# A streaming encoder layer on one Trainium2 core: a reordered LoRA, stores and loads on other queues, two-input work moved between engines, and a new step table

## The chip, the core and the metric

One core of one Trainium2 chip. The core has a matrix engine (TensorE, "PE" in the profile; its weight loads are "PEld"), a vector engine (VectorE, "DVE"), an activation engine (ScalarE, "ACT"), a general engine (GpSimd, "POOL") and a queue engine for transfers (SyncE, "SP"). ACT and POOL can issue transfers too; an engine takes its instructions in order, issues of transfers included, and "ACTq", "POOL ... DMA" or "SPq" in a row is such an issue. The metric is the device time of one execution in microseconds (us), lower is better.

## The reference, cut to what matters

One layer works on 1056 token rows (1024 of a prompt, 32 of running streams). One input projection feeds three mixers, whose outputs are concatenated, projected, normalised, and followed by an MLP.

```python
proj = x @ prm['w_in']
q_lat, kv_lat, k_rope_raw, u, p_rwkv = jnp.split(proj, IN_SPLITS, axis=-1)
mla_out, ckv, krope = mla_mixer(q_lat, kv_lat, k_rope_raw, pos, ckv_past, krope_past, prm)   # 6 heads
s5_out, s5_state = s5_mixer(u, s5_x0, s5_block_len, prm)
rwkv_out, rwkv_state, shift = rwkv_mixer(p_rwkv, shift0, rwkv_s0, prm)                       # 6 heads x 64
merged = jnp.concatenate([mla_out, s5_out, rwkv_out], -1)                                    # 384 | 256 | 384
x = layer_norm(ALPHA * x + merged @ prm['w_out'], ...)
x = layer_norm(ALPHA * x + jnp.square(jax.nn.relu(x @ prm['w_up'])) @ prm['w_down'], ...)

# in rwkv_mixer: a LoRA of three parts (32, 32 and 64 inner columns)
w_log = -jax.nn.softplus(-(prm['w0'] + jnp.tanh(wd) @ prm['w_w2'])) - 0.5
a = jax.nn.sigmoid(prm['a0'] + ad @ prm['w_a2'])
g = jax.nn.sigmoid(gd) @ prm['w_g2']
...
bonus = jnp.sum(r * k * prm['r_k'], -1, keepdims=True) * v
y = (y + bonus.reshape(b, t, RWKV_W)) * g
# in s5_mixer
z = jax.nn.gelu(y);  out = z * jax.nn.sigmoid(z @ prm['w_glu'] + prm['b_glu'])
# in mla_mixer: q = rms_norm(q_lat) @ w_qb; 64 plain ("nope") and 32 rotated ("rope") columns a head
```

## The kernel before

**Numbers.** Most products are made in three passes over a value split in a high and a low part: `split3` (L45 to L50) copies the high part on ScalarE (L49) and subtracts it on VectorE, or on an engine given as `lo_eng` (L50); `mm3` (L59 to L67) multiplies hi by hi (L63), lo by hi (L65) and hi by lo (L67).

**Input stage (0 to some 270 us).** Tiles of 128 columns of the input projection (`in_proj`, results "acc") run in turn, each over three blocks of 384, 384 and 288 tokens. `stage_lora` computes, for each of three pairs of RWKV heads and each of three blocks (384, 384, 290 columns), a gate (64 rows of weights, bank "pti") and the two 32-row products `w` and `a` (banks "fs" or "pt"), each in three passes (L308). A chain of `issue_after` fixes the order gate, w, a in every pass. ScalarE empties the banks with sigmoids (L310 to L313). After the last sigmoid ScalarE changes its function table (L76), and `front_k` (L351 to L403, VectorE and ScalarE) and the triangular inverse (`rwkv_inv`, L770 to L826) follow. `stage_kv_in`, `stage_kr`, `stage_q_in`, `stage_u` and `stage_q` finish the projections. `stage_q` (L1169) makes the queries and stores them in DRAM as `q_d`, per head 64 nope rows (`nope(p)` for heads 2p and 2p+1, L1182, from ScalarE) and 32 rope rows (L1196 and L1204, from POOL). After it the "shift" output (`sho`) is transposed and stored (L2263 to L2266).

**The middle (some 270 to 690 us).** Four generators are interleaved: F (`attn_front`: keys, query loads, score maxima), O (`attn_back`: values, scores, softmax times values), S (the inverse's end, then the RWKV scan in nine tiles of 128 tokens) and X (`stage_s5`). The string `PLAN` gives the order: each letter lets one generator run to its next `yield`. The function `middle` ties the TensorE instructions of a step behind those of the step before (`mark`), so TensorE's order is the table's; the other engines' orders come from the compiler's own schedule, made with estimated times. What the prediction touches here: `attn_setup` clears and copies key tiles on POOL (L1111 to L1118) and zeroes 32 rows of the two query pairs `q2` on ScalarE (L1120); `attn_keys` (L1128) makes the keys of two heads from one bank at a time; `attn_q` (L1212) loads a head's query from `q_d` and splits it; `attn_max` takes the maxima of the scores (L1235, L1236); in `attn_out`, `ptk` clears on POOL (L1292) precede the `av` products (L1265), and L1270 to L1278 finish a block. In the scan, `rwkv_pairs` (L863, L864) and `rwkv_norm` (L1003, L1004) have two POOL instructions each. In `stage_s5`, the results are written to `z_d` (L673), read back in another layout by sixteen loads on SP (L688), and passed through the GELU on ScalarE (L693).

**Output projection (some 640 to 790 us).** `out_early` loads and splits three token tiles (384 columns) of the merged results `mg_d` with POOL while attention runs out. The last attention store is put in `g.late` (L814) and issued after it (L2288). Then come six more tiles: `out_load` (L1452) loads `mraw` and splits it with POOL, `out_mm` multiplies, `out_ln` and `out_turn` normalise and transpose. The MLP fills the rest of the time; nothing of it is changed.

Of the kernel before, what the change touches and what calls it, by code (L numbers as in the profile page):

```python
# [277 lines left out]
def stage_lora(g):  # L278
# [15 lines left out]
    for p in PAIRS:  # L294
        cs = slice(p * P, p * P + P)
        nc.gpsimd.memset(g.cs65[:, p, 0:1040].rearrange("p (c x) -> p c x", x=65)[:, :, 0:1], 0.0)
        nc.gpsimd.memset(g.cs65[:, p, 1040:1041], 0.0)
        nc.gpsimd.memset(g.at[:, p, 1024:1026], 0.0)
        gt = g.lq.tile([P, WSH], F32, tag="o", name="gt", bufs=2)
        for i, (s, n) in enumerate(HB):  # L300
            pool, tag = ((g.pfs, "fs"), (g.pt, "pt"))[(p + i) % 2]
            w, a = (pool.tile([P, 512], F32, tag=tag, name=tag)[:, :n] for _ in range(2))
            gate = g.pti.tile([P, 512], F32, tag="pti", name="pti")[:, :n]
            mm = None
            for j, (l, r) in enumerate(((wh_, ah), (wh_, al), (wl_, ah))):
                for z, rows in ((gate, slice(64, 128)), (w, slice(0, 32)), (a, slice(32, 64))):
                    with g.tc.issue_after(mm.ins) if mm is not None else nullcontext():
                        mm = nc.tensor.matmul(out=z, lhsT=l[rows, cs], rhs=r[rows, s:s + n], start=j == 0, stop=j == 2)  # L308
# [304 lines left out]
def stage_s5(g):  # L613
# [72 lines left out]
    for h in range(2):  # L686
        for i in range(8):
            nc.sync.dma_start(out=zv[16 * i:16 * i + 16, h], in_=g.z_d[8 * h + i].rearrange("(t c) k -> c t k", c=16))  # L688
# [297 lines left out]
def rwkv_norm(g, t):  # L986
# [16 lines left out]
    nc.gpsimd.tensor_tensor(out=yc, in0=yc, in1=g.bn.pop(t), op=ALU.add)  # L1003
    nc.gpsimd.tensor_tensor(out=yc, in0=yc, in1=gate, op=ALU.mult)  # L1004
# [148 lines left out]
def stage_q(g):  # L1153
# [24 lines left out]
    def nope(p):
        q = f("qnope")
        product(q, wa[:, :, 2 * p:2 * p + 2].rearrange("p k h c -> p k (h c)"))  # L1180
        for h in range(2):
            nc.scalar.dma_start(out=g.q_d[2 * p + h, 0:64], in_=q[hsl(h)])  # L1182
# [12 lines left out]
    for h in range(4):  # L1195
        nc.gpsimd.dma_start(out=g.q_d[h, 64:96], in_=qa[32 * h:32 * h + 32])  # L1196
# [135 lines left out]
def middle(g, scan):  # L1332
# [39 lines left out]
    "FFFFFFFFFFFSFFFFFFSFFSFFFFFFFFFSFFFFSOOSOFSOOOSFOOSOOSOOSFSOSFOFOOOOOSSXOOOFSFOOSXOOOOFOOOSFFSSSOSSO"  # L1372
    "OXFFXFOSFOFOSOSXFFFOOFSOSSOSXOOSFSFSOOFSXOOSOFOFOSXSOOSFOOFXOXOSFOFSOOOOSFOFOSXOSSOOOFSOOXFSFOOSFFFS"
    "FXSFFFFSFFXSOOSFOSOOFOOOOSXFSSSOOXFOSOOSOOFXOOSOOFOOSXSSOFOOFOSOXOSSOOOOFOSXOFFSOXSFFSSFFFSFFSOOXSOS"
    "FFXSSFOOSOOOXOSOOOFSOOOOOSFOOSOFSXOOOFSSOXSOFFOOSFOOSXOOFSOSFXOOOOSSFOFSXFFFSFFFSFFFXSFFSFFSOOXOOSOS"
    "OOFSOXOSFFOSOSOXOFSOOFSOXOOSSXOSFOFOOOOOOOSFSSSOXSFOOOOSFOXFOXOSOSFOFOSSSFFSFFFFOOOOSOOOSOOOSOOOSOSS"
    "OOSSOOSOSFOSOOOOOOOOOOOOOOO"
# [806 lines left out]
def tile_trunk(ctx, tc, a, o):  # L2184
# [31 lines left out]
    with ExitStack() as s1:  # L2216
# [49 lines left out]
        nc.scalar.dma_start(out=g.o["sh_s"], in_=sho[10:20])  # L2266
# [146 lines left out]
```

## Time and profile before

| | us |
|---|---|
| median of 3 runs (lowest, highest) | 1465.21 (1462.29, 1467.37) |
| the profiled execution | 1463.32 |
| its span, first to last instruction | 1461.2 |
| busy: TensorE | 1381.3 (95%) |
| busy: VectorE | 970.7 (66%) |
| busy: ScalarE | 656.0 (45%) |
| busy: GpSimd | 161.9 (11%) |
| mean granted TensorE clock | 0.978 |

The page of the profile gives busy shares and the chain of work that ended last. The other views are of the same execution: stretches of the span with every engine's busy time, the timeline of one engine (start, length, engine, line, operation, written tile, read tiles, shapes, count; in brackets the idle time before and what ended it), and the list of waits (who waited for whom: total, times, longest). TensorE's matmuls are pipelined: its pace is read from starts, not lengths.

### The profile page before, as it was taken

What the parts mean: (1) busy time and instruction counts of PE and PEld (TensorE: products, weight loads), DVE (VectorE), ACT (ScalarE), POOL (GpSimd) and SP (SyncE); (2) the same over time, 40 slices, a digit from 0 to 9 for tenths busy, and PEclk for the clock granted to TensorE, in tenths of its full rate; (3) what the DMA queues carried; (4) which work ended last, traced back from release to release, by engine and by line L of the source; (5) the groups of instructions that cost most, each with busy time, mean ns of one, the idle gap of its engine ahead of it and who ended that gap; (6) DMA issues with size and microseconds to landing.
All of it is one profiled execution on the core that took longest, in us unless ns stands there. A gap on an engine that the chain in (4) does not pass through costs nothing.

```text
span 1461.2 us, 28203 instructions
## 1 busy us (share of the span) xinstructions
PE 1381.3 (95%) x11532; PEld 1236.2 (85%) x11532; DVE 970.7 (66%) x1735; ACT 656.0 (45%) x1143; POOL 161.9 (11%) x278
## 2 busy tenths in 40 slices
PE   9999999799989979889899899999999999999996
PEld 9978888476776757666589899999999999999996
DVE  7675979655664745652858976666656786665477
ACT  6546544335553645542326444344444344434432
POOL 1211110401111111210530000000000000000022
PEclk9999999899998999989999999999999999999998
DMA  5433563671343321131633344444429785354232
GB/s 202 146 123 135 168 172 87 168 138 50 92 107 87 82 60 35 64 108 44 214 119 131 136 181 139 162 142 147 137 87 385 256 306 187 90 172 131 70 101 76
DMA packets 150325, 198.58 MB, mean 136 GB/s; under 512 B 53392, under 2 KB 98116, under 8 KB 149688
## 3 DMA queue, kind: packets, MB, share of 16 engines
q1 hardware_dynamic: 129396, 175.91, 37.7%
q10 hardware_dynamic: 20448, 19.88, 4.5%
q8 instruction: 90, 1.47, 0.4%
q0 software_dynamic: 352, 1.01, 0.3%
q14 instruction: 39, 0.32, 0.1%
HBM read 129.42 MB, written 67.28 MB: 135 GB/s over the span
## 4 chain that ended last, share of the span: by engine, by line
PE 75%; DVE 9%; DMA 6%; ACT 4%; issue 2%; SPq 2%; ACTq 1%; POOL 1%; DVEq 0%; POOLq 0%
PE acc L63 19%; PE acc L67 19%; PE acc L65 19%; PE av L1265 3%; PE sc L63 1%; DMA mraw<-mg_d 1%; DVE mx L1236 1%; PE st L63 1%; DMA wo<-in_w_out 1%; PE st L65 1%; PE st L67 1%; PE scv L1147 1%; PE scq L1169 1%; PE pti L308 1%; PE sc L67 1%
## 5 line engine op out<-in xcount | busy, mean ns | idle before, releaser
L63 PE MATMUL acc<-xo,wo 128*128 128x272 f32 (+1 forms) x896 | 254.0, 284 | 2.8 <-ACT wo L49 2.8
L67 PE MATMUL acc<-xo,wo 128*128 128x256 f32 (+1 forms) x896 | 253.2, 284 | 1.6 <-DVE wo L50 1.6
L65 PE MATMUL acc<-xo,wo 128*128 128x272 f32 (+1 forms) x896 | 253.0, 283 | 0.0
L67 PE MATMUL acc<-hop,wo 128*128 128x272 f32 (+1 forms) x896 | 194.4, 284 | 0.0
L63 PEld LDWEIGHTS acc<-xo,wo 128*128 128x128 f32 x896 | 168.1, 188 | 3.0 <-ACT wo L49 3.0
L67 PEld LDWEIGHTS acc<-xo,wo 128*128 128x128 f32 x896 | 167.9, 188 | 2.0 <-DVE wo L50 2.0
L65 PEld LDWEIGHTS acc<-xo,wo 128*128 128x128 f32 x896 | 168.5, 188 | 0.0
L63 PE MATMUL acc<-hop,wo 128*128 128x256 f32 (+1 forms) x768 | 159.1, 285 | 0.0
L65 PE MATMUL acc<-hop,wo 128*128 128x272 f32 (+1 forms) x768 | 158.3, 283 | 0.0
L67 PEld LDWEIGHTS acc<-hop,wo 128*128 128x128 f32 x896 | 142.4, 188 | 0.0
L65 PE MATMUL acc<-xl,wmhi 128*128 128x384 f32 (+3 forms) x384 | 126.8, 330 | 0.7 <-DVE xl L50 0.7
L67 PE MATMUL acc<-xh,wmlo 128*128 128x384 f32 (+3 forms) x384 | 126.1, 329 | 0.0
L63 PE MATMUL acc<-xh,wmhi 128*128 128x384 f32 (+3 forms) x384 | 125.8, 328 | 0.3 <-ACT xh L49 0.3
L65 PEld LDWEIGHTS acc<-hop,wo 128*128 128x128 f32 x768 | 119.6, 189 | 0.0
L63 PEld LDWEIGHTS acc<-hop,wo 128*128 128x128 f32 x768 | 118.7, 188 | 0.0
L49 ACT ACTIVATE wo<-wr 128x512 fp32r<-128x512 f32 (+1 forms) x64 | 46.9, 738 | 117.6 <-PE acc L67 70.2
L2150 POOL TENSOR_TENSOR wr<-wr,gb 128x512 f32<-128x512 f32 (+1 forms) x12 | 17.2, 1453 | 667.7 <-ACT wr L2148 667.7
L1265 PE MATMUL av<-ptk,vo 128*128 128x512 f32 (+5 forms) x204 | 75.1, 452 | 11.7 <-ACT po L1270 8.1
L50 DVE TENSOR_TENSOR hop<-hraw,hop 128x1056 fp32r<-128x1056 f32 (+3 forms) x58 | 70.4, 1213 | 14.4 <-ACT hop L49 14.3
L50 DVE TENSOR_TENSOR wo<-wr,wo 128x512 fp32r<-128x512 f32 (+1 forms) x64 | 52.3, 821 | 40.7 <-ACT wo L49 40.6
L49 ACT ACTIVATE hop<-hraw 128x1056 fp32r<-128x1056 f32 (+3 forms) x58 | 60.6, 1045 | 30.2 <-PE acc L67 28.9
L65 PEld LDWEIGHTS acc<-xl,wmhi 128*128 128x128 f32 (+1 forms) x384 | 70.8, 184 | 3.9 <-DVE xl L50 1.3
(552 smaller groups left out, 3071.6 us busy)
## 6 DMA issues: line engine op xcount, KB each, us to landing
hraw<-h_d SPq DMA_DIRECT2D x48, 528.0 KB
wr<-in_w_up SPq DMA_DIRECT2D x35, 512.0 KB
h_d<-hx SPq DMA_DIRECT2D x16, 792.0 KB
h_d<-ht SPq DMA_DIRECT2D x16, 792.0 KB
wd<-in_w_dn SPq DMA_DIRECT2D x16, 512.0 KB
wr<-in_w_dn SPq DMA_DIRECT2D x16, 512.0 KB
ld<-rw SPq DMA_DIRECT2D x24, 320.0 KB
wmraw<-in_w_m SPq DMA_DIRECT2D x12, 512.0 KB
```

The source lines that it names most:

```text
L49: nc.scalar.activation(out=hi, in_=ps, func=AF.Copy)
L50: (lo_eng or nc.vector).tensor_tensor(out=lo, in0=ps, in1=hi.bitcast(F32), op=ALU.subtract)
L63: nc.tensor.matmul(out=outs[i], lhsT=lh, rhs=rhs[i][0], start=start, stop=False, **kw)
L65: nc.tensor.matmul(out=outs[i], lhsT=lh, rhs=rhs[i][1], start=False, stop=False, **kw)
L67: nc.tensor.matmul(out=outs[i], lhsT=ll, rhs=rhs[i][0], start=False, stop=stop, **kw)
L308: mm = nc.tensor.matmul(out=z, lhsT=l[rows, cs], rhs=r[rows, s:s + n], start=j == 0, stop=j == 2)
L1147: nc.tensor.matmul(out=ps[:n, j], lhsT=c, rhs=g.wkv[:, 1, p * P:p * P + P], start=True, stop=True)
L1169: nc.tensor.matmul(out=ps, lhsT=w[:, k], rhs=g.qn[:, k, s:s + n], start=k == 0, stop=k == 1)
L1236: nc.vector.tensor_reduce(out=mx[:n, t, b // 512:b // 512 + 1], in_=ps[:n, :w], axis=AX.X, op=ALU.max)
L1265: nc.tensor.matmul(out=po[:, c:n], lhsT=vo[:w, kt].rearrange("p a x -> p (a x)")[:, 64 * i:64 * i + P], rhs=pt[:w, c:n], start=kt == tiles ...
L2150: nc.gpsimd.tensor_tensor(out=o[:n, c], in0=o[:n, c], in1=g.gb2[:n, 0, c], op=ALU.mult)
```

## The change

- LoRA: in each of the nine groups the three passes of `w` and `a` are issued first, then the three of the gate, tied behind them.
- S5: the second eight of the sixteen loads of `z_d` are issued by POOL, and two more `yield`s stand before the GELU.
- The four POOL instructions of the scan, the low parts of `out_load`, and four clears in `attn_setup` go to VectorE.
- Only the first query pair is zeroed in `attn_setup`; the second is zeroed when head 1 loads its query.
- `attn_first_keys` replaces `attn_keys` for heads 0 and 1: four products into four banks, then the splits of head 0, then head 0's query, then the splits of head 1.
- Query stores: nope rows of heads 0 and 1 on SP, of heads 2 to 5 on POOL; rope rows of heads 0 to 3 on SP. The nope tiles lie in the memory of the input's low part.
- The last attention store is issued by ScalarE. The shift output is made ahead of `stage_u` and stored from SP.
- A new `PLAN` (526 letters for 527: three F steps fewer, two X steps more).

```diff
-            mm = None
-            for j, (l, r) in enumerate(((wh_, ah), (wh_, al), (wl_, ah))):
-                for z, rows in ((gate, slice(64, 128)), (w, slice(0, 32)), (a, slice(32, 64))):
-                    with g.tc.issue_after(mm.ins) if mm is not None else nullcontext():
-                        mm = nc.tensor.matmul(out=z, lhsT=l[rows, cs], rhs=r[rows, s:s + n], start=j == 0, stop=j == 2)
+            low = ((wh_, ah), (wh_, al), (wl_, ah))
+            for j, (l, r) in enumerate(low):
+                for z, rows in ((w, slice(0, 32)), (a, slice(32, 64))):
+                    mm = nc.tensor.matmul(out=z, lhsT=l[rows, cs], rhs=r[rows, s:s + n], start=j == 0, stop=j == 2)
+            for j, (l, r) in enumerate(low):
+                with g.tc.issue_after(mm.ins):
+                    mm = nc.tensor.matmul(out=gate, lhsT=l[64:128, cs], rhs=r[64:128, s:s + n], start=j == 0, stop=j == 2)
...
-            nc.sync.dma_start(out=zv[16 * i:16 * i + 16, h], in_=g.z_d[8 * h + i].rearrange("(t c) k -> c t k", c=16))
+            (nc.sync, nc.gpsimd)[h].dma_start(out=zv[16 * i:16 * i + 16, h], in_=g.z_d[8 * h + i].rearrange("(t c) k -> c t k", c=16))
...
+    yield
+    yield
     yield
     yield
     log_exp_table(g, [nc.scalar.activation(out=zt, in_=zt, func=AF.Gelu_apprx_tanh)], False)
...
-    nc.gpsimd.tensor_tensor(out=x, in0=ld[:, :, 2, :w], in1=ld[:, :, 4, :w], op=ALU.mult)
+    nc.vector.tensor_tensor(out=x, in0=ld[:, :, 2, :w], in1=ld[:, :, 4, :w], op=ALU.mult)
...
-    nc.gpsimd.tensor_tensor(out=yc, in0=yc, in1=g.bn.pop(t), op=ALU.add)
+    nc.vector.tensor_tensor(out=yc, in0=yc, in1=g.bn.pop(t), op=ALU.add)
...
-        for x in g.q2[i] if i < 2 else ():
+        for x in g.q2[i] if i < 1 else ():
...
+def attn_first_keys(g):
+    nc = g.nc
+    parts = []
+    for j, (src, o, n) in enumerate(((g.ckv[:, 0:512], 0, 512), (g.ckv[:, 512:TP], 512, 512), (g.cpast, 1024, 512), (g.ckv[:, TP:T], 1536, 32))):
+        pool, tag = ((g.psc, "sc"), (g.pst, "st"))[j % 2]
+        ps = pool.tile([P, 512], F32, tag=tag, name="sck")
+        nc.tensor.matmul(out=ps[:, :n], lhsT=g.wkv[:, 0, 0:P], rhs=src, start=True, stop=True)
+        parts.append((ps, o, n))
+    yield
+    for i in range(2):
+        for ps, o, n in parts:
+            split3(g, ps[hsl(i), :n], g.kh[i][0:64, o:o + n], g.kl[i][0:64, o:o + n])
+        yield
+        yield
...
-            nc.scalar.dma_start(out=g.q_d[2 * p + h, 0:64], in_=q[hsl(h)])
+            (nc.gpsimd if p else nc.sync).dma_start(out=g.q_d[2 * p + h, 0:64], in_=q[hsl(h)])
...
-        nc.gpsimd.dma_start(out=g.q_d[h, 64:96], in_=qa[32 * h:32 * h + 32])
+        nc.sync.dma_start(out=g.q_d[h, 64:96], in_=qa[32 * h:32 * h + 32])
...
-            store(g, nc.sync if h == 5 and s == 512 else None, g.mg_d[h // 2, :, s:s + n], ot[:, s:s + n])
+            store(g, nc.scalar if h == 5 and s == 512 else None, g.mg_d[h // 2, :, s:s + n], ot[:, s:s + n])
...
-        if h % 2 == 0:
+        if h == 0:
+            keys = attn_first_keys(g)
+            for _ in range(3):
+                next(keys)
+                yield
+        elif h % 2 == 0:
             yield from attn_keys(g, h // 2)
         g.qs[h] = yield from attn_q(g, h)
+        if h == 0:
+            yield from keys
...
-        split3(g, raw[:, k], mh[:, k], ml[:, k], g.nc.gpsimd)
+        split3(g, raw[:, k], mh[:, k], ml[:, k])
```

More of the change, by code (lines that the diff above doesn't have):

```diff
@@ L862, in rwkv_pairs @@
     x = r[:, :, K_NV].rearrange("q p h x -> q p (h x)")[:, :, :w]
-    nc.gpsimd.tensor_tensor(out=x, in0=ld[:, :, 2, :w], in1=ld[:, :, 4, :w], op=ALU.mult)
-    nc.gpsimd.tensor_tensor(out=x, in0=x, in1=bc(g.vec[:, V_RK:V_RK + 3][:, :, None], [P, 3, w]), op=ALU.mult)
+    nc.vector.tensor_tensor(out=x, in0=ld[:, :, 2, :w], in1=ld[:, :, 4, :w], op=ALU.mult)
+    nc.vector.tensor_tensor(out=x, in0=x, in1=bc(g.vec[:, V_RK:V_RK + 3][:, :, None], [P, 3, w]), op=ALU.mult)
     ps = g.pr.tile([P, 3, P], F32, tag="pr", name="prk")[:, :, :w]
@@ L1002, in rwkv_norm @@
         nc.vector.tensor_scalar(out=yc[:, p], in0=yc[:, p], scalar1=g.vec[:, V_GNG + p:V_GNG + p + 1], scalar2=g.vec[:, V_GNB + p:V_GNB + p + 1], op0=ALU.mult, op1=ALU.add)
-    nc.gpsimd.tensor_tensor(out=yc, in0=yc, in1=g.bn.pop(t), op=ALU.add)
-    nc.gpsimd.tensor_tensor(out=yc, in0=yc, in1=gate, op=ALU.mult)
+    nc.vector.tensor_tensor(out=yc, in0=yc, in1=g.bn.pop(t), op=ALU.add)
+    nc.vector.tensor_tensor(out=yc, in0=yc, in1=gate, op=ALU.mult)
     s = TP if s == SOFF else s
@@ L1110, in attn_setup @@
     for x in (kr, g.kpast):
-        nc.gpsimd.memset(x[96:128], 0.0)
-        nc.gpsimd.memset(x[96:97], -1.0)
+        nc.vector.memset(x[96:128], 0.0)
+        nc.vector.memset(x[96:97], -1.0)
     for x, o, c, n in ((g.kpast, TP, 0, 512), (kr, 0, 0, TP), (kr, 1536, TP, TS)):
@@ L1177, in stage_q @@
             nc.scalar.dma_start(out=wr[:, k, j, x:x + 32 * n].rearrange("p (h c) -> p h c", c=32), in_=g.a["w_qb"][:, k, h:h + n, c:c + 32])
+    qs_ = g.xp.tile([P, KD, T], F32, tag="xl", name="qnope")
     def nope(p):
-        q = f("qnope")
+        q = qs_[:, KD - 3 + p]
         product(q, wa[:, :, 2 * p:2 * p + 2].rearrange("p k h c -> p k (h c)"))
         for h in range(2):
-            nc.scalar.dma_start(out=g.q_d[2 * p + h, 0:64], in_=q[hsl(h)])
+            (nc.gpsimd if p else nc.sync).dma_start(out=g.q_d[2 * p + h, 0:64], in_=q[hsl(h)])
     cs, sn = f("ropec"), f("ropes")
@@ L1212, in attn_q @@
     nc.sync.dma_start(out=q[0:96], in_=g.q_d[h])
-    if h > 1:
+    if h > 0:
         for x in (qh, ql):
@@ L1371 @@
 PLAN = (
[L1372 to L1377, printed above, removed]
+    "FFFFFFFFSFSFFSFFFFFFSFFFFFFFFFFFSFOOSOFSOOOSFOOOSSOSOOSFSOFOFOOOOOOSXOSOOFSFOSXOOOOFOOOSFFSSSOSSOOXF"
+    "FXFOSFOFOSOSXFFFOOFSOSSOSXOOSFSFSOOFSOFXXOSOFOFOOOOSOFSSOFOXOOXFSOOOFOFOOSOXSSSOOSOFSOFXSFSFOOFFSSFX"
+    "FFFSFFFSXOOSFOOSOFOOSOOXFSSOOSXFOSOOSOOSFXOOOOFOOXOSFSSOOFSSOXOSOOOOOFOSXOFFSOXSFSFFSFFSFFSOOXSOSFFX"
+    "SSFOOSOOOXOSOOOFSOOOOOFSOFOOSOOXSOFSSOXOFOOSFXXFOXOSSOOFSOSFXOOOOSSFOFSXFFFSFFFFSFFFSXFFFSFFSOXOOSSO"
+    "OFSOXOSFFOSOSOXOFSOOFSOXFOSOSXOSFOOOSOOOOOFSSOSXSFOOOOSFOXFOXOSOSFOFOSSSFFSFFOOSSOOOOOOOOOOSOOOOSOFS"
+    "SOSSOOOOSSOSOOOOOOOOOOOOOO"
 )
@@ L2223, in tile_trunk @@
         g.wpool = s1.enter_context(tc.tile_pool(name="wpool", bufs=2, reuse_waits="tile"))
-        xp = s1.enter_context(tc.tile_pool(name="xp", bufs=1, reuse_waits="tile"))
+        xp = g.xp = s1.enter_context(tc.tile_pool(name="xp", bufs=1, reuse_waits="tile"))
         g.xh = xp.tile([P, KD, T], F32R, tag="xh", name="xh")
@@ L2258, in tile_trunk @@
         stage_q_in(g)
-        stage_u(g)
-        stage_q(g)
-        sho = g.p1.tile([32, P], F32, tag="kk", name="sho", bufs=3)
+        sho = g.p1.tile([P, 9, 32], F32, tag="krt", name="sho", bufs=1).rearrange("p a b -> p (a b)")[:, :P]
         ps = g.pti.tile([P, P], F32, tag="pti", name="pti")
@@ L2264, in tile_trunk @@
         nc.scalar.activation(out=sho[:20], in_=ps[:20], func=AF.Copy)
-        nc.scalar.dma_start(out=g.o["sh_p"], in_=sho[0:10])
-        nc.scalar.dma_start(out=g.o["sh_s"], in_=sho[10:20])
+        nc.sync.dma_start(out=g.o["sh_p"], in_=sho[0:10])
+        nc.sync.dma_start(out=g.o["sh_s"], in_=sho[10:20])
+        stage_u(g)
+        stage_q(g)
         s2.close()
```

## The prediction

> **What bounds the kernel now.** I read the page first, then stretches of the span, then what TensorE waited for. The page: the span, TensorE's busy share, the chain.
>
> ```profile
> span 1461.2 us, 28203 instructions
> PE 75%; DVE 9%; DMA 6%; ACT 4%; issue 2%; SPq 2%; ACTq 1%; POOL 1%; DVEq 0%; POOLq 0%
> ```
>
> Three quarters of the chain that ended last is TensorE at work, so an edit pays where it shortens TensorE's own stream or closes a hole in it. The columns of the next view are length, busy time (instructions) of PE, PEld, DVE, ACT, POOL, then granted clock, DMA share, GB/s.
>
> ```profile
> 0.00:270.00 270.00, 263.63 (x1691) 231.62 (x1692) 208.55 (x433) 146.71 (x251) 47.74 (x108) 1.00 0.45 145
> 270.00:300.00 30.00, 18.45 (x270) 13.62 (x270) 16.30 (x37) 4.76 (x11) 5.42 (x8) 0.77 0.97 222
> 300.00:690.00 390.00, 350.57 (x3738) 263.49 (x3732) 212.72 (x461) 187.02 (x388) 57.78 (x122) 0.95 0.29 76
> 690.00:790.00 100.00, 95.17 (x479) 75.45 (x479) 71.12 (x103) 34.63 (x91) 33.81 (x28) 0.98 0.46 147
> 790.00:1461.20 671.20, 653.52 (x5371) 652.00 (x5369) 462.00 (x703) 282.90 (x404) 17.18 (x12) 0.99 0.47 162
> ```
>
> The MLP (the last row) holds nothing that is changed. Ahead of it TensorE is idle 6.4 us before 270, 11.6 us in 270 to 300 (at a clock of 0.77), 39.4 us in the interleaved middle, 4.8 us in the output projection: 62 us, the pool from which the gaps below can be closed. Two of its largest waits (the other two stand in parts 3 and 5):
>
> ```profile
> PE sc L63 <- ACT qh L49: 7.0, 1, 7.0
> 621.44 0.24 PE L63 MATMUL sc<-kh,qh 128*32 128x32 f32 x1 [5.55 <-DVE mx L1236]
> ```
>
> All four have an edit aimed at them. Before 270 TensorE is full, and there only the LoRA order can win.
>
> **1. LoRA order: -5 us (0 to -7.2).**
>
> ```profile
> 79.16 0.34 PE L67 MATMUL acc<-xh,wmlo 128*128 128x384 f32 x1
> 79.33 0.34 PE L63 MATMUL acc<-xh,wmhi 128*128 128x384 f32 x1
> 96.44 0.44 PE L308 MATMUL pti<-lah,wh 64*128 64x384 f32 x1
> 96.81 0.44 PE L308 MATMUL fs<-lah,wh 32*128 32x384 f32 x2
> 98.66 0.44 PE L67 MATMUL acc<-xh,wmlo 128*128 128x384 f32 x1
> 103.85 0.40 PE L308 MATMUL pti<-lah,wll 64*128 64x290 f32 x1
> 104.18 0.40 PE L308 MATMUL pt<-lah,wll 32*128 32x290 f32 x2
> 152.10 0.66 PE pt L325 x2
> 153.34 1.23 DVE fc L351 x2
> ```
>
> Starts tell the pace. Gate (64 rows) and pair (two of 32 rows, "x2", side by side) alternate, six blocks of 0.37 us: 96.44 to 98.66 is 2.22 us for nine matmuls. Neighbours of one shape and the same 384 columns start 0.17 us apart. The new order is three pairs, then three gates: two blocks follow another shape (0.37), four follow their own. At 0.17 a group takes 1.42, 0.80 less. The 290-column groups run at 0.33; scaled by 290/384 the floor is 0.13, again 0.80 less. Nine groups: -7.2 us. If a change of shape costs nothing and the block itself does, nothing is won: 0. A loss is excluded, since no change of shape is added. The 0.17 row is nearest in columns and dtype, but it has one strip of weights to load where a pair has two, so I take the saving at 6.3 in TensorE's stream. TensorE carries the chain up to 152.10, then DVE; DVE's scans behind the LoRA also wait for other DVE work, and so 5 of it reach the end.
>
> [...]
>
> **2. Query stores, first keys, zeroing of the second query pair: -6 us (-2 to -9).**
>
> ```profile
> 269.17 1.69 ACTq L1182 DMA_DIRECT2D q_d<-qnope  x2
> 270.93 2.09 ACTq L2266 DMA_DIRECT2D out_sh_s<-sho  x1
> 274.70 2.16 ACTq L1182 DMA_DIRECT2D q_d<-qnope  x2
> 276.91 1.18 ACT L49 ACTIVATE qh<-q 96x512 fp32r<-96x512 f32 x2 [2.08 <-issue]
> 247.82 1.08 ACT L1120 ACTIVATE qh<-ckv 32x1056 fp32r<-32x1056 f32 x1
> 252.39 1.24 PE L1169 MATMUL scq<-qn,wqr 128*128 128x288 f32 x4 [1.86 <-ACT qrope L1170]
> SPq L1212 <- DMA q_d<-qrope: 23.3, 1, 23.3
> 264.67 2.15 POOL L1196 DMA_DIRECT2D q_d<-qrope  x4
> ```
>
> ScalarE issues the six nope stores and the shift output in line with its arithmetic. Four nope stores and one shift store stand between 269.17 and 276.86 and take 5.9 us; behind them waits the split of head 0's query, for which TensorE idles 7.0 us. With the nope stores on SP (2) and POOL (4) and the shift output ahead of stage_u on SP, that split comes 5.9 us sooner, at 271.0, if head 0's query is there. It is loaded behind the rope store (SP's 23.3 us), and POOL, busy with copies of the keys, came to that store at 264.67 and took 2.15 us to issue it. On SP it needs no POOL. Dropping two of four zeroing activations (1.08 each) from ScalarE also relieves the 1.86 us wait at 252; they come back in head 1's load, where ScalarE is idle. Four banks for the first keys put head 0's splits ahead of head 1's; that is inside the same hole. Against it: SP now holds two nope and four rope stores, each waiting for its producer, and the scan's inverse loads, the query loads and the `ld` loads queue behind them; POOL's four stores stand ahead of its `ld` and `xt` clears. DMA is at 0.97 of its engines in 270 to 300, so the next thing late is the scan's loads. Ends: everything closes (7.0 + 1.9 = 8.9) or only the zeroing's 1.9. Nearer the first: -6.
>
> **3. S5's reload on two queues: -3.5 us (+1 to -8).**
>
> ```profile
> 504.59 4.03 SPq L688 DMA_DIRECT2D zt<-z_d  x8
> 509.44 4.18 SPq L688 DMA_DIRECT2D zt<-z_d  x8
> 515.37 1.28 ACT L693 ACT_TABLE_LOAD   x1 [4.50 <-DMA zt<-z_d]
> 520.68 2.07 PE L1265 MATMUL av<-ptk,vo 128*128 128x512 f32 x2 [7.32 <-ACT po L1270]
> ```
>
> Sixteen loads take SP until 513.6; the GELU waits 4.50 us for them with ScalarE's queue behind it, and TensorE 7.32 us. POOL issues a store in 0.54 us (2.15 for 4), SP a load in 0.51: eight each, side by side, are issued by 509, so the wait falls by some 4 us and the table load (1.28) and the GELU itself stay. The two added yields move nothing by themselves: in the old table the loads' and GELU's X steps have 18 steps of the other streams between them, and in the new one 18 again. I take 3.5. Low end: TensorE's whole 7.3 plus the slow `av` behind it. High end: POOL's loads wait for the tile to be free, and a `ptk` clear behind them is late.
>
> **4. GpSimd's two-input work on VectorE: -1.5 us (+4 to -5).**
>
> ```profile
> 616.08 1.44 POOL L1003 TENSOR_TENSOR yc<-yc,bn 128x384 f32<-128x384 f32 x1
> 498.19 1.00 POOL L1004 TENSOR_TENSOR yc<-yc,gate 128x384 f32<-128x384 f32 x1
> 494.10 0.56 DVE L1000 TENSOR_TENSOR yc<-yc,iv 128x384 f32<-128x384 f32 x1
> 614.90 1.76 DVE L1276 TENSOR_TENSOR rt<-rt,rec 64x512 f32<-64x512 f32 x1 [0.90 <-ACT rec L1274]
> 638.05 0.69 DVE L1276 TENSOR_TENSOR rt<-rt,rec 64x512 f32<-64x512 f32 x1 [0.31 <-ACT rec L1274]
> 642.29 1.23 DVE L50 TENSOR_TENSOR wo<-wo 128x1024 fp32r<-128x1024 f32 x1 [1.52 <-ACT wo L49]
> 731.20 2.69 POOL L50 TENSOR_TENSOR ml<-mraw,mh 128x640 fp32r<-128x640 f32 x3 [2.14 <-ACT mh L49]
> ```
>
> Nine scan tiles with four instructions each: 36 x 1.00 us leave POOL, 36 x 0.56 = 20.2 us come to DVE, which is 55% busy in 300 to 690. While POOL works on two inputs the same DVE instruction takes 1.76 instead of 0.69: that is part of the 5.55 us hole at 621, before which two `yc` instructions ran on POOL; `out_early` keeps its splits there, so a part stays. Cover gone, the 20.2 us would be in DVE's queue ahead of the score maxima. The six later output tiles move 2.69 us each from POOL to about 1.3 on DVE (8 us in all) while TensorE is full in 710 to 790; hidden. The four clears in attn_setup: hidden.
>
> **5. Last attention store on ScalarE's queue: -4.5 us (0 to -6).**
>
> ```profile
> SPq L2288 <- DVE ot L1278: 32.7, 1, 32.7
> 695.86 2.92 SPq L1452 DMA_DIRECT2D mraw<-mg_d  x3
> 704.09 0.69 PE L63 MATMUL acc<-wo,mh 128*32 128x512 f32 x2 [4.83 <-ACT mh L49]
> ```
>
> SP stands 32.7 us at this store, and the residual, gains and next tile's loads behind it; TensorE then idles 4.83 us. Tile 8's columns were stored long before, so its loads may leave as soon as their memory is free. On ScalarE nothing waits behind the store until that split. If the memory is freed only at attention's end, 0.
>
> **The new table: 0 (+10 to -10).** It sets TensorE's order for 280 to 690. Its second to fourth S steps come 5, 5 and 8 steps sooner once the three saved F steps are taken off; the rest is nearly the old one.
>
> **Sum.** 5 + 6 + 3.5 + 1.5 + 4.5 = 20.5. The profiled execution took 1463.3 us, its span 1461.2 and 2.1 around it; 1463.3 - 20.5 = 1442.8, so 1443. The median of the runs shown is 1465.2, 1.9 higher, inside their spread.
>
> **Rivals.**
> [...]
> - Transfers hide parts 1 and 2: DMA is at 0.97 from 270 to 300, and the S steps that now stand earlier wait there for the inverse's loads, TensorE's whole stream behind them. Then 11 us go and 9.5 remain: 1454. Against: SP stood 23.3 us at one wait ahead of those loads, so a queue and not the bytes made them late.
> - The gains and new waits cancel: 1462.
> - Slower: the table was made for estimated times; TensorE takes its steps strictly in order, so a step whose operand is late holds all others. The middle loses 39.4 us so now. It decides when its 132 S steps wait 0.19 us more each (25 us); at 0.21 (27.5 us) the time is 1470. For it: 36 more DVE instructions sit in that stream. Against: ends of chains in the middle get shorter, DVE is half idle.
>
> **How the numbers follow.** 0.3% is 4.4 us, about what this kernel's measurement tells from no change. Forecast 0.57 (own range 1434 to 1451), weights rule 0.13, transfers 0.13, cancelled 0.08, slower 0.09. Faster 0.83, same 0.08, slower 0.09. The five parts' low ends together give 1428; the range leaves off that corner and the two last cases: 1430 to 1458.
>
> **What would show it.** Right: L308 blocks of one shape under 0.25 us apart; no ACTq store between the `qnope` copies, and the first `sc` before 272 less LoRA's gain; the GELU's wait under 1 us; no `mx` wait over 3 us near 610; the idle before tile 8's first `acc` gone. Wrong: the first S step's matmuls waiting on `zb`, POOL's `ptk` clears late near 510, or more than 40 us idle in the middle.

## The result and the profile after

The changed kernel takes 1448.3 us (median of four runs, 1446.2 to 1450.7) against 1463.9 for the kernel before beside it: ratio 0.9891, interval 0.9871 to 0.9912, some 16 us less. Forecast was 1443 (1430 to 1458). The profiled execution took 1446.2, against 1463.3 before: 17.1 less, where the sum said 20.5. Total and sign came out, but the gain does not sit where the prediction put it.

The page of the changed kernel, its span and chain:

```profile
span 1444.5 us, 28201 instructions
PE 81%; DVE 9%; ACT 4%; DMA 2%; issue 2%; SPq 1%; POOL 0%; ACTq 0%; DVEq 0%; POOLq 0%
```

TensorE's share of the chain went from 75 to 81%, transfers from 6 to 2%. The same stretches as shown of before (busy time of PE, PEld, DVE, ACT, POOL; granted clock, DMA share, GB/s). Work has moved ahead of these fixed boundaries:

```profile
270.00:300.00 30.00, 22.39 (x387) 17.39 (x385) 21.28 (x47) 7.71 (x14) 11.71 (x12) 0.75 0.69 137
300.00:690.00 390.00, 357.08 (x3673) 267.49 (x3668) 234.15 (x518) 191.97 (x406) 28.19 (x96) 0.96 0.34 88
690.00:790.00 100.00, 98.36 (x557) 81.88 (x556) 75.78 (x117) 40.06 (x94) 11.15 (x9) 0.99 0.38 122
```

Idle TensorE time fell from 11.6 to 7.6 us, from 39.4 to 32.9 and from 4.8 to 1.6. Shares cannot say which edit did that. The start of the same product in both traces can; the last column is how far the changed kernel is ahead:

| TensorE product | before | after | ahead |
|---|---|---|---|
| first `scq` (queries) | 243.25 | 241.13 | 2.1 |
| last `scq` | 270.22 | 262.19 | 8.0 |
| first `sc` (scores) | 277.59 | 275.72 | 1.9 |
| first `av` | 310.99 | 306.11 | 4.9 |
| fourth head's `scm` | 482.79 | 471.28 | 11.5 |
| `av` behind the GELU's hole | 520.68 | 509.86 | 10.8 |
| sixth head's `scm` | 622.47 | 606.52 | 16.0 |
| last `av` | 688.54 | 671.65 | 16.9 |
| 1401st `acc` (output projection) | 733.27 | 714.57 | 18.7 |
| last `pt` | 1449.80 | 1432.58 | 17.2 |

By the sum it should have been 5 ahead at the first `scq`, 11 at the first `sc`, 14.5 to 16 behind the GELU and 20.5 in the output projection. It was 2, 2, 11 and 18.7; between the first `av` and the sixth `scm` it won 11 us, where parts 3 and 4 were to bring 5. These are starts of single executions, and the first rows of this one are late by its clock: it ran at 0.50 for 3.41 us from 90.33 and again from 172.25, which takes up to 1.7 us each. Six of the kernels below are the same up to the first `sc`; they start the first `scq` at 238.2 to 239.5 and the first `sc` at 272.8 to 274.1, so 3.7 to 5.1 and 3.5 to 4.8 ahead. TensorE's largest waits now (total, times, longest), and a row of its timeline:

```profile
PE av L1289 <- ACT ptk L1314: 9.0, 2, 8.0
PE sc L63 <- DVE mx L1260: 7.7, 12, 1.6
...
PE sc L63 <- DVE kl L50: 4.9, 1, 4.9
```

```profile
606.52 0.38 PE L1267 MATMUL scm<-ident,m 128*9 128x128 f32 x1 [3.28 <-DVE m L1265]
```

The 5.55 us at `mx` are gone (longest 1.6), but at the same head's next product, `scm`, 3.28 us stand where 0.68 stood before. The holes at the first `sc` (4.9) and at the GELU (8.0) are still there.

### The profile page after: what moved, and what is told of

It is laid out like the page before. It is cut to its first block, busy times and chain, and to the rows that moved or that the text cites. A ratio compares the mean times of both kernels' runs of the same rounds, so it can differ in the third digit from the quotient of the medians.

```text
span 1444.5 us, 28201 instructions
## 1 busy us (share of the span) xinstructions
PE 1378.9 (95%) x11532; PEld 1238.2 (86%) x11532; DVE 981.1 (68%) x1793; ACT 656.6 (45%) x1143; POOL 114.9 (8%) x228
## 4 chain that ended last, share of the span: by engine, by line
PE 81%; DVE 9%; ACT 4%; DMA 2%; issue 2%; SPq 1%; POOL 0%; ACTq 0%; DVEq 0%; POOLq 0%
PE acc L63 20%; PE acc L67 20%; PE acc L65 20%; PE av L1289 3%; PE scq L1191 1%; DMA wo<-in_w_out 1%; DVE mx L1260 1%; PE st L63 1%; PE sc L63 1%; PE st L65 1%; PE st L67 1%; PE scv L1169 1%; PE prw L896 1%; DVE xo L50 1%; PE pti L802 1%
## 5 line engine op out<-in xcount | busy, mean ns | idle before, releaser
L1289 PE MATMUL av<-ptk,vo 128*128 128x512 f32 (+5 forms) x204 | 74.5, 450 | 10.3 <-ACT ptk L1314 9.0
L63 PEld LDWEIGHTS acc<-xh,wmhi 128*128 128x128 f32 (+1 forms) x384 | 71.7, 187 | 5.2 <-ACT ckv L204 1.9
L67 PEld LDWEIGHTS acc<-xh,wmlo 128*128 128x128 f32 (+1 forms) x384 | 71.7, 187 | 3.5 <-issue 1.6
```

Source lines behind the costliest of these rows:

```text
L63: nc.tensor.matmul(out=outs[i], lhsT=lh, rhs=rhs[i][0], start=start, stop=False, **kw)
L67: nc.tensor.matmul(out=outs[i], lhsT=ll, rhs=rhs[i][0], start=False, stop=stop, **kw)
L1289: nc.tensor.matmul(out=po[:, c:n], lhsT=vo[:w, kt].rearrange("p a x -> p (a x)")[:, 64 * i:64 * i + P], rhs=pt[:w, c:n], start=kt == tiles ...
```

## The experiments

Ratios are against the kernel before, run in the same set on the same chip; its medians there were 1460.7 to 1462.9. One per mille is 1.5 us, and an interval reaches about 3 to 4 us to either side, so that the difference of two kernels by their ratios is uncertain by some 4 to 5 us. The traces are single executions: the one of the kernel before took 1463.3, 0.4 to 2.6 us more than those medians. The theory to test was the prediction's: each part is worth its own term. Its rival came from the table above: the new step table, set at 0, won the middle.

**LoRA alone.** Kernel before, new LoRA order.

```diff
-                for z, rows in ((gate, slice(64, 128)), (w, slice(0, 32)), (a, slice(32, 64))):
+                for z, rows in ((w, slice(0, 32)), (a, slice(32, 64))):
...
+            for j, (l, r) in enumerate(low):
+                with g.tc.issue_after(mm.ins):
+                    mm = nc.tensor.matmul(out=gate, ...)
```

> The kernel before with the LoRA order alone. The prediction's term: 6.3 us less in TensorE's stream, 5 of it at the end, so 1459. What the changed kernel's trace suggests: its LoRA blocks take 4.4 us less from start to start, but its first query product starts only 2.1 us sooner, so 1462. [...]

Measured: median 1459.3, ratio 0.9989 (0.9969 to 1.0008). In its trace the first `scq` is 5.1 us ahead (238.15 for 243.25) and the first score block 7.1 (270.49 for 277.59). Of that 8.6 are there at the last `av` and 5.8 at the end, more than the 1.6 of the ratio: the traced execution (1457.5) lies 1.8 us below this kernel's median, and that of the kernel before 2.6 above its median in this set. So how much of the lead is kept stays open. The holes at the GELU (7.1) and at `mx` (4.9) stay.

**Scan work back on GpSimd.** Changed kernel, four instructions.

```diff
-    nc.vector.tensor_tensor(out=x, in0=ld[:, :, 2, :w], in1=ld[:, :, 4, :w], op=ALU.mult)
+    nc.gpsimd.tensor_tensor(out=x, in0=ld[:, :, 2, :w], in1=ld[:, :, 4, :w], op=ALU.mult)
...
-    nc.vector.tensor_tensor(out=yc, in0=yc, in1=gate, op=ALU.mult)
+    nc.gpsimd.tensor_tensor(out=yc, in0=yc, in1=gate, op=ALU.mult)
```

> The changed kernel with the four scan instructions of part 4 back on GpSimd. The changed kernel is 4.9 us ahead at the first av product, 11.5 ahead near 475 us and 17 ahead at the last av; something in the middle gave 12 us that the prediction put mostly elsewhere. If it is the relief of VectorE from GpSimd's two-input work, this kernel loses 6 to 11 us: 1454 to 1459. If it is the table, or the two together only, it loses the 1.5 of the prediction at most: 1448 to 1450, with the same stretched VectorE instructions (1.76 for 0.69 us) as before.

Measured: 1447.5, 0.9909 (0.9882 to 0.9936): not to be told from the changed kernel.

**Old table in the changed kernel**, its first three F steps dropped, and two yields ahead of the GELU instead of four.

```diff
-    "FFFFFFFFSFSFFSFFFFFFSFFFFFFFFFFFSFOOSOFSOOOSFOOOSSOSOOSFSOFOFOOOOOOSXOSOOFSFOSXOOOOFOOOSFFSSSOSSOOXF"
...
+    "FFFFFFFFSFFFFFFSFFSFFFFFFFFFSFFFFSOOSOFSOOOSFOOSOOSOOSFSOSFOFOOOOOSSXOOOFSFOOSXOOOOFOOOS"
...
```

> The changed kernel with the old step table (three early F steps dropped, since the first keys have three fewer; the two added yields ahead of the GELU taken out, so that the GELU keeps its old place). If the middle's 12 us come from the table: 1455 to 1460. If they come from part 4: 1447 to 1450. The prediction set the table at 0.

Measured: 1455.5, 0.9959 (0.9940 to 0.9977): 7 us above the changed kernel by the medians, 10 by the ratios. One row of TensorE's timeline in this kernel, then one of the list of waits in the kernel with the scan work on GpSimd:

```profile
617.75 0.23 PE L63 MATMUL sc<-kh,qh 128*32 128x32 f32 x1 [6.77 <-DVE mx L1258]
```

```profile
PE sc L63 <- DVE mx L1260: 6.3, 10, 1.6
```

With the old table the hole at `mx` is back (6.77) although the scan work is on VectorE; with the new table it is gone (longest 1.6) although that work is on GpSimd. The table closes it, not part 4. From the first to the sixth `scm` the three traces with the old table take 322.9 to 326.2 us, the eleven with the new one 308.5 to 317.7: the middle's gain is the table's.

**New table in the kernel before**, with `FFF` put in front and the two added yields.

```diff
-    "FFFFFFFFFFFSFFFFFFSFFSFFFFFFFFFSFFFFSOOSOFSOOOSFOOSOOSOOSFSOSFOFOOOOOSSXOOOFSFOOSXOOOOFOOOSFFSSSOSSO"
...
+    "FFFFFFFFFFFSFSFFSFFFFFFSFFFFFFFFFFFSFOOSOFSOOOSFOOOSSOSOOSFSOFOFOOOOOOSXOSOOFSFOSXOOOOFOO"
...
```

> The kernel before with the new step table (three F steps put in front, and the two yields ahead of the GELU added, so that every letter meets the step it was written for). If the table alone gives the middle's 12 us: 1452 to 1458. If it needs the other parts: 1462 to 1466. If strict order ties TensorE to later operands, slower than 1468.

Measured: 1459.6, 0.9991 (0.9973 to 1.0009): nothing that can be told from noise. Its trace shows what it loses at the start (TensorE's and then SP's timeline):

```profile
277.49 0.47 PE L63 MATMUL sc<-kh,qh 128*128 128x128 f32 x1 [7.63 <-ACT qh L49]
...
280.32 0.28 PE L800 MATMUL pti<-zb,n 32*32 32x32 f32 x2 [1.64 <-DMA zb<-zt_d]
...
290.67 0.80 PE L63 MATMUL sc<-kh,qh 128*128 128x512 f32 x1 [3.83 <-DVE mx L1238]
```

```profile
273.69 7.48 SPq L789 DMA_DIRECT2D zb<-zt_d  x4
```

The table sets the scan's inverse earlier, its first product then waits for loads that SP reaches only at 273.69, and the first head's `scm` starts 6.0 us later than before (303.39 for 297.37). In the changed kernel these loads leave at 264.02. The earlier scan steps need the new queues. The middle itself gains as much as in the changed kernel: from the first to the sixth `scm` it takes 310.9 us (before 325.1, changed kernel 311.7). From there to the 1401st `acc` it loses 3.0 again (113.8 for 110.8). In this trace 5.2 us are left at the end, 1 by the medians; the traced execution (1457.5) lies 2.2 us below its median.

**Old store queues in the changed kernel.**

```diff
-            (nc.gpsimd if p else nc.sync).dma_start(out=g.q_d[2 * p + h, 0:64], in_=q[hsl(h)])
+            nc.scalar.dma_start(out=g.q_d[2 * p + h, 0:64], in_=q[hsl(h)])
...
-        nc.sync.dma_start(out=g.q_d[h, 64:96], in_=qa[32 * h:32 * h + 32])
+        nc.gpsimd.dma_start(out=g.q_d[h, 64:96], in_=qa[32 * h:32 * h + 32])
```

> The changed kernel with the query stores on their old queues (nope rows issued by ScalarE, rope rows by GpSimd), all else kept. Theory: the new table moves scan steps to the front of the middle, and they need the inverse's loads, which stand on SP behind the query load; with the old stores that load waits for GpSimd's rope stores again, the inverse's loads leave near 274 instead of 264, TensorE waits for them as in the run with the new table alone (2.2 us) and for head 0's query (7 us): 1453 to 1456. Rival: the stores are worth only what the first score block showed (1.9 us sooner): 1449 to 1450.

Measured: 1456.6, 0.9972 (0.9950 to 0.9995), 8 to 12 us above the changed kernel. From the last `scq` (258.72) to the first `sc` (276.63) pass 17.9 us, in the changed kernel 13.5: 4.4 of it is seen at this place. The expected cause is only half right: GpSimd, no longer busy with the keys, issues its rope stores from 248.63 on already, and the inverse's loads leave at 267.5, not at 274. Where the rest of the 8 to 12 us lies the trace does not show; its execution (1453.3) is 3.3 us below this kernel's median.

**Old LoRA order in the changed kernel.**

```diff
-            for j, (l, r) in enumerate(low):
-                for z, rows in ((w, slice(0, 32)), (a, slice(32, 64))):
...
+                for z, rows in ((gate, slice(64, 128)), (w, slice(0, 32)), (a, slice(32, 64))):
```

> The changed kernel with the old LoRA order. The prediction's term: 5 us lost, 1453. What LoRA alone gave to the kernel before (1.6 us, interval -1.2 to 4.5): 1450. [...] By the traces the LoRA blocks take 4.4 us more of TensorE's stream, and the first query product would start 2 to 4.5 us later.

Measured: 1453.4, 0.9948 (0.9926 to 0.9971): 5 us above the changed kernel by the medians, 8 by the ratios. So beside the other parts the order is worth what was forecast or more; alone it gave 1.6, with an upper end of 4.5. Its first `scq` starts at 242.63. The kernel with the last store on SP (below) differs up to there by the LoRA order alone, and starts it at 238.19; neither trace has a slow stretch of the clock ahead of it. So the whole 4.4 us of the blocks arrive there.

**S5's reload on SP alone.**

```diff
-            (nc.sync, nc.gpsimd)[h].dma_start(out=zv[16 * i:16 * i + 16, h], in_=...)
+            nc.sync.dma_start(out=zv[16 * i:16 * i + 16, h], in_=...)
```

> The changed kernel with all sixteen reload transfers of S5 on SP again, the added yields and the table kept. The prediction: issuing bounds the reload, so the hole at the GELU grows from 8.0 to about 11.5 us: 1451.5. A rival from the traces: in the changed kernel the sixteen loads take 11.5 us from the first issue (493.09) to the GELU's start (504.63), before it was 10.8 (504.59 to 515.37), so the transfers themselves bound and the queues don't matter: 1448. A third, from the run with the new table alone, where sixteen loads on SP left a hole of only 2.7 us: the split on two queues is what costs, 1443.

Measured: 1445.4, 0.9893 (0.9871 to 0.9915): no loss. From the timelines of the changed kernel: SP's issues, GpSimd's, then ScalarE's GELU and the `av` behind it:

```profile
493.09 3.18 SPq L690 DMA_DIRECT2D zt<-z_d  x7
...
496.78 0.43 SPq L690 DMA_DIRECT2D zt<-z_d  x1
...
493.62 4.23 POOL L690 DMA_DIRECT2D zt<-z_d  x8 [5.91 <-PE av L1289]
...
504.63 1.28 ACT L697 ACT_TABLE_LOAD   x1 [6.39 <-DMA out_s_s<-so]
...
509.86 2.08 PE L1289 MATMUL av<-ptk,vo 128*128 128x512 f32 x2 [8.00 <-ACT ptk L1314]
```

The row of the table load names the store of the S5 state, but what the GELU reads is `zt`, and by the trace the last of GpSimd's loads landed at 504.27. So with two queues the transfers set the landing: the last issue is over at 497.85, and the GELU starts 6.8 us later. On one queue issues and transfers keep pace: before, the GELU started 1.8 us behind the last issue (513.62), here on SP alone 2.1 (501.89 to 504.03), while of GpSimd's loads in the changed kernel none lands sooner than 3.1 us after its issue. From first issue to landing 11.5 us pass with two queues, before it was 10.8, and here, on SP alone, 10.3 (493.70 to 504.03). The split shortened the issuing from 9 us to 4.8, and the transfers took longer. The rows of the DMA queues in 493 to 505 (packets, MB, share of the 16 engines), SP's and GpSimd's in the changed kernel, then SP's in this one:

```profile
q1 hardware_dynamic: 1296, 0.81, 44.1%
q0 software_dynamic: 256, 0.55, 31.2%
```

```profile
q1 hardware_dynamic: 2448, 1.35, 48.1%
```

The same bytes cost 75% of the engines' time in place of 48. Whether GpSimd's queue or two queues at once make it so was not tried. The wait went from 4.50 to 6.39 because ScalarE is there earlier (at 498.24, 5.2 us behind the first issue, before 6.3) and the landing is 0.7 later.

**GELU two X steps later.**

```diff
+    yield
+    yield
     log_exp_table(g, [nc.scalar.activation(out=zt, in_=zt, func=AF.Gelu_apprx_tanh)], False)
-    yield
-    yield
```

> The changed kernel with two yields moved from behind the GELU to ahead of it, so that the GELU stands two X steps later and nothing else moves (its result is first used near 543 us, the GELU ends at 508). If ScalarE's wait of 6.4 us for the reload makes the hole of 8.0 us: the wait goes, 3 us of hole remain for the two table loads and the GELU itself, 1443. If the hole comes with those 4.5 us of ScalarE's time wherever they stand: 1445 to 1446. If the work behind becomes late in its place: 1448.

Measured: 1447.3, 0.9906 (0.9881 to 0.9930). Not a test of the hole after all: the GELU kept its place in ScalarE's queue, right behind the store of the S5 state, waited 6.13 us there, and the hole is 7.7. Yields move the table's mark on TensorE; ScalarE's order is the compiler's, from estimated times.

**GELU tied** behind the ScalarE work traced ahead of it.

```diff
-    log_exp_table(g, [nc.scalar.activation(out=zt, in_=zt, func=AF.Gelu_apprx_tanh)], False)
+    with g.tc.issue_after(last_traced(g, mybir.EngineType.Activation)):
+        log_exp_table(g, [nc.scalar.activation(out=zt, in_=zt, func=AF.Gelu_apprx_tanh)], False)
```

> The changed kernel with the GELU (and its table loads) tied behind the last ScalarE instruction that was traced ahead of it, so that twelve ScalarE instructions of the other streams, ptk copies among them, now stand ahead of it; with yields alone it kept its place in ScalarE's queue. If the hole of 8.0 us is ScalarE standing at the reload with those copies behind it: no wait for the reload, at most 3 us of hole from the GELU's own 4.5 us, 1443. If the hole moves to another late operand: 1448.

Measured: 1439.7, 0.9863 (0.9838 to 0.9889), 4 us below the changed kernel by the ratios, whose intervals overlap, and 9 by the medians. ScalarE's timeline at that place, and an `av` of TensorE's beside the GELU:

```profile
503.92 0.60 ACT L1315 ACTIVATE ptk<-st 128x512 f32<-128x512 f32 x1 [0.55 <-PE st L67]
...
511.52 1.28 ACT L698 ACT_TABLE_LOAD   x1
512.82 1.98 ACT L698 ACTIVATE zt<-zt 128x2128 f32<-128x2128 f32 x1
...
512.10 1.13 PE L1290 MATMUL av<-ptk,vo 128*128 128x512 f32 x2
```

No wait stands before the table load, and TensorE's timeline has no idle time from 496 to 516.5. The GELU's own 4.5 us on ScalarE cost TensorE nothing here. From the fourth to the fifth head's `scm` pass 66.5 us, and 66.5 again in the last kernel below, which has the same tie; in the changed kernel 73.8, in its other variants with the new table 73.2 to 76.4. So the tie wins some 7 us at this place; by the ratios of the whole time that is not clear of noise.

**Last attention store back on SP.**

```diff
-            store(g, nc.scalar if h == 5 and s == 512 else None, ...)
+            store(g, nc.sync if h == 5 and s == 512 else None, ...)
```

> The changed kernel with the last attention store back on SP. The prediction: 4.5 us slower, 1452.5, with an idle time of 4 to 5 us before tile 8's first acc product. What the changed kernel's trace suggests: it won only 0.4 us in the output projection, since the wait of 4.83 us was followed there by two others (0.5 before acc, 1.75 before pt) and by a granted clock near one half for 3 us; 1448 to 1449.

Measured: 1448.7, 0.9910 (0.9889 to 0.9932), within the noise. TensorE in this kernel (first row), and in the changed one:

```profile
689.53 1.06 PE L63 MATMUL acc<-wo,mh 128*32 128x512 f32 x2 [6.42 <-ACT mh L49]
```

```profile
681.42 0.65 PE L63 MATMUL acc<-wo,mh 128*32 128x512 f32 x2 [0.47 <-ACT mh L49]
...
684.29 1.97 PE L1562 MATMUL pt<-ident,z 128*128 128x128 f32 x8 [1.75 <-DVE z L1543]
...
688.62 1.05 PE L65 MATMUL acc<-wo,mh 128*32 128x512 f32 x2
```

One wait of 6.42 becomes 0.47, 1.75 and 0.65 (before an `ml`), and two products, like those of the last row, take 0.85 us there until 690.3 and 0.47 later. From the last `av` to the 1401st `acc` pass 42.9 us, with the store on SP 46.0: 3 us in the traces, 0.5 (medians) to 3 (ratios) in the time.

**Zeroing of the query pairs on GpSimd**, in the setup.

```diff
-        for x in g.q2[i] if i < 1 else ():
-            nc.scalar.activation(out=x[96:128], in_=g.ckv[96:128], func=AF.Copy, scale=0.0)
+        for x in g.q2[i] if i < 2 else ():
+            nc.gpsimd.tensor_scalar(out=x[96:128], in0=g.ckv[96:128], scalar1=0.0, scalar2=None, op0=ALU.mult)
...
-    if h > 0:
+    if h > 1:
```

> The changed kernel with the zeroing of both query pairs in the setup and on GpSimd. In the changed kernel four zeroing activations (4.1 us) stand in ScalarE's queue ahead of the last key split of head 0 and the first score block starts at 275.72. If ScalarE's queue bounds the start of attention: that block at 272, 1444 to 1445. If the inverse's loads bound (the last of the eight is issued at 272.5, TensorE's first product with them stands one score block behind): the block moves but the time does not, 1447 to 1448.

Measured: 1446.5, 0.9897 (0.9874 to 0.9921), not to be told from the changed kernel. The block starts at 272.57 and the first `scm` at 297.62, 2.8 later than in the changed kernel: GpSimd needs 2.9 to 3.6 us for each zeroing that ScalarE did in 1.1, the fourth ends at 276.6, head 1's query split waits for it until 276.62, and head 0's maxima stand behind that split on VectorE (TensorE idle 4.76 us).

**GELU tied, reload on SP, zeroing on VectorE**: the first two as above, both pairs zeroed in the setup as in the run before, and

```diff
-            nc.scalar.activation(out=x[96:128], in_=g.ckv[96:128], func=AF.Copy, scale=0.0)
+            nc.vector.tensor_scalar(out=x[96:128], in0=g.ckv[96:128], scalar1=0.0, scalar2=None, op0=ALU.mult)
```

> The changed kernel with three edits that the runs point to: the GELU tied behind the other streams' ScalarE work, all sixteen reload transfers of S5 on SP, and both query pairs zeroed in the setup on VectorE, which is idle there, in place of ScalarE. If ScalarE's 4 us of zeroing bound the start of attention: first score block 3 to 4 us sooner, at most 2 us of it lost to the inverse's loads, 1435 to 1438 (GELU tied alone 1439.7). If head 1's query load, which stands in VectorE's queue ahead of head 0's maxima, is next: 1439 to 1441.

Measured: 1442.0, 0.9861 (0.9835 to 0.9887), the same as with the GELU tied alone. VectorE zeroes in 0.70 us each, ScalarE is free of it, and yet the first `sc` is only 1.0 us sooner (272.58 for 273.57). Its row:

```profile
272.58 0.47 PE L63 MATMUL sc<-kh,qh 128*128 128x128 f32 x1 [7.99 <-DVE kl L50]
```

Next in the way are VectorE's key splits: the one of `kpast` took 2.01 us at 267.06, in the changed kernel 0.69. GpSimd copies keys from 265.25 to 268.53; whether that is the cause was not tried.

## Why the prediction was right, and where it was not

**Part 1, LoRA: -5, right in size, one step wrong.** TensorE's timeline in the changed kernel: a pair side by side ("x2"), then a group whose `w` and `a` came apart:

```profile
69.06 0.45 PE L307 MATMUL fs<-lah,wh 32*128 32x384 f32 x2
69.34 0.34 PE L307 MATMUL fs<-lal,wh 32*128 32x384 f32 x2
69.52 0.33 PE L307 MATMUL fs<-lah,wll 32*128 32x384 f32 x2
69.78 0.44 PE L65 MATMUL acc<-xl,wmhi 128*128 128x384 f32 x1
...
94.67 0.44 PE L307 MATMUL pt<-lah,wh 32*128 32x384 f32 x1
...
96.02 0.44 PE L310 MATMUL pti<-lah,wh 64*128 64x384 f32 x1
...
96.74 0.43 PE L307 MATMUL pt<-lah,wh 32*128 32x384 f32 x1
```

The block behind one of its own strips takes 0.18, the first and the last of the three 0.28 and 0.26, none 0.37. Three take 0.72 (69.06 to 69.78), so a group with its pair side by side takes 1.44: the forecast 1.42. But `w` and `a` are no longer tied to each other, and in four of the nine groups, all from 76 us on, the compiler set other products between them, as above (94.67 and 96.74). Such a pair pays its 0.7 us twice: 2.8 us in all. From start to start, summed over all LoRA rows, the blocks went from 19.6 to 15.2 us, 4.4 less; with the 2.8 it would have been the 7.2 of the working, and the term was 6.3. Tying the pair was not tried. The end with 0 is out: a block behind one of its own 32-row strips takes 0.18 us, as full height does (0.17), and taking the order out cost 5 to 8 us. The weights rule, which has 0.13 of the chances, is shown by no run; what the runs show in its place is the 0.18.

**Part 2, stores and first keys: -6, the place wrong.** No store stands on ScalarE, the 1.86 us before the query product are gone, and the last `scq` came 8 us sooner; but the LoRA order alone also removes the 1.86, and brings the last `scq` 7.2 us sooner (262.99). Before, the past keys' transposes and the key products (3.6 us of TensorE) ran between the query products, and now all of them follow the last `scq`. This is the compiler's order, not the queue: with the old stores the load of `ct` leaves at 240.61 instead of 255.63, and the transposes still follow. ScalarE's queue behind them, in the changed kernel:

```profile
263.06 1.08 ACT L1124 ACTIVATE qh<-ckv 32x1056 fp32r<-32x1056 f32 x1
...
266.33 0.60 ACT L1092 ACTIVATE cpast<-sct 128x512 f32<-128x512 f32 x1
...
270.73 1.08 ACT L1239 ACTIVATE qh<-kh 32x1056 fp32r<-32x1056 f32 x1
...
272.80 1.91 ACT L49 ACTIVATE kh<-sck 64x512 fp32r<-64x512 f32 x4
```

The second pair's zeroing, said to come back "where ScalarE is idle", stands at 270.73 ahead of head 0's last key split; that step was false by 2.1 us. So the first `sc` won 1.9 us (3.5 to 4.8 in the six kernels that are the same up to there), where parts 1 and 2 together were to bring 11, and 275.72 stands against "before 272". The LoRA order alone has it at 270.49, and the changed kernel without that order at 277.22, before 277.59: at this place part 2 gave 0.4 us without part 1 and cost 2 to 5 with it. What the queues also did, the prediction had named as a danger and not as a gain: the inverse's loads leave at 264.02 instead of 274.42, and on them the table depends.

**Part 3, reload: -3.5, wrong.** The failed step is that the landing follows the issues: that eight and eight loads, issued 4 us sooner, would land 4 us sooner. On one queue the landing does stand right behind the last issue (1.8 us), as the prediction read; on two it came 6.8 us behind, and the reload took 11.5 us for 10.8. The GELU's wait grew from 4.50 to 6.39, where it was to be below 1, and undoing the split cost nothing. The added yields were to move nothing by themselves, and when two more were put ahead of the GELU it kept its place.

**Part 4: -1.5, nothing measurable** for the scan instructions (undone: 0.8 faster by medians, 2.6 slower by ratios). The low parts of `out_load` and the four clears were not put back by themselves. The hole at `mx` was tied to this part, and the table closed it. The reading behind it was wrong too: the instruction of 1.76 us at 614.90 began beside a split of `out_early` on GpSimd (kernel before, first row), and the scan's `yc` came to GpSimd only at 616.08. With the old table and the scan work on VectorE it takes 1.75 again, beside such a split (other rows). So taking the scan work off GpSimd does not remove the stretch:

```profile
614.29 1.82 POOL L50 TENSOR_TENSOR ml<-mraw,mh 128x768 fp32r<-128x768 f32 x1 [2.31 <-ACT mh L49]
```

```profile
610.21 4.02 POOL L50 TENSOR_TENSOR ml<-mraw,mh 128x768 fp32r<-128x768 f32 x2 [3.08 <-ACT mh L49]
...
610.82 1.75 DVE L1298 TENSOR_TENSOR rt<-rt,rec 64x512 f32<-64x512 f32 x1 [1.73 <-ACT rec L1296]
```

Nor was the added work on VectorE hidden everywhere: the 3.28 us before the sixth `scm` are 0.68 with the scan work on GpSimd, where two other waits (1.43 and 2.40) stand a little later instead.

**Part 5: -4.5, mis-sized.** The wait went, as forecast, and is worth 0.5 to 3, within the noise: the next transposes wait 1.75 for VectorE's `z`, and from 685 to 691 TensorE runs at a clock of 0.50.

**The table: 0, wrong, 7 to 10 us in this kernel** and 1 in the old one (up to 3.9 by its interval), where its 14 us of the middle are lost in part ahead of it and behind it. The prediction had looked only at its first scan steps and called the rest "nearly the old one".

So the total came out by compensation, which is luck: parts 3, 4 and 5 were to bring 9.5 us and, undone one by one, gave -3 in sum by the medians and 6 by the ratios, each within the noise, and the table, at 0, is worth 7 to 10. Nor can the parts be added. Taken out one by one, LoRA, the stores and the table cost 5, 8 and 7 us by the medians and 8, 12 and 10 by the ratios, 20 or 30 together, more than the 16 of the whole; put in alone, LoRA and the table gave 1.6 and 1. For the table the two differ by more than the noise of the ratios; for LoRA, whose own trace shows 5.8 alone, it stays open. Of the rivals, "transfers hide" had the right mechanism, scan steps that wait for the inverse's loads; it is what happens to the table without the new queues.

## What to carry to other kernels

Lay the starts of the same product in both traces side by side before believing a sum that came out; take an edit out of the changed kernel as well as putting it alone into the old one, since an earlier step is worth nothing while its operand is late (the table alone gave 1 us, in the changed kernel it is worth 7 to 10). A landing that stands right behind the last issue does not say that issuing on two queues makes it earlier: here only the run without the split told (10.3 us from first issue to landing, with two queues 11.5). A wait in front of a long instruction with the work of other streams behind it in the same queue can be closed by tying that instruction behind their work; here that closed the hole of 8.0 us, and asking for its operand on two queues did not (8.0 where 7.3 stood before). A start read from one execution can be off by the clock, here by up to 1.7 us for each 3.41 us at 0.50: look at the granted clock ahead of it, and at a second trace of the same code.
